# A transformer kernel: shift and scale of the second norm multiplied out on GpSimd in place of TensorE and VectorE

## The chip, the core and the metric

The kernel runs on one core of a Trainium2 chip. Its engines work side by side, each through its own queue in a fixed order, and wait for one another by semaphores: TensorE (PE, with its weight loads shown apart as PEld), VectorE (DVE), ScalarE (ACT), GpSimd (POOL) and SyncE (SP), whose queue issues the weight transfers. The metric is the device time of one launch in microseconds (us), as the median of repeated runs.

## What is computed

Two transformer blocks over 256 tokens of width 1024, all in 32-bit floats. The part that matters here is the modulation of the first block: a vector `c` gives six rows of 1024 numbers, and the fourth and fifth (index 3 and 4) are shift and scale of the second norm, which stands ahead of the mixture of experts.

```
mod = silu(c) @ w_ada + b_ada
shift1, scale1, gate1, shift2, scale2, gate2 = split(mod, 6)
h  = rms_norm(x, norm1_g) * (1 + scale1) + shift1
q, k, v, ..., g_sb, g_mb = split(h @ w_in)
x  = x + gate1 * ((sigmoid(g_sb) * (o_sb @ w_branch_sb) + sigmoid(g_mb) * (o_mb @ w_branch_mb)) @ w_out)
h2 = rms_norm(x, norm2_g) * (1 + scale2) + shift2
x  = x + gate2 * moe_ffn(h2)          # router, 64 experts, a shared expert
```

After it come a norm and the second block (two feed-forward parts around a mixing part), which the change doesn't touch.

## The kernel before

The first block's dense part is `phase_a`. Its matrix products are split into a high and a low part on both sides: for each 128-row chunk of a weight matrix, ACT rounds it (wH, L125), DVE subtracts (wL, L126), and PE multiplies three times (L116 to L118). The results of the projections are the tiles `pslt` (transposed) and `pslin`.

One part of the modulation is a product of a 1024-vector with a 1024 x 1024 matrix. `ada_half(q, j, E)` (L367) makes half of it, 512 columns: it loads the 512 columns of `w_ada` as two tiles `wada` of four chunks each, and then takes one of two ways. For every q but 4, PE multiplies (L383): 8 products of a chunk with a stationary tile `cpad` that holds silu(c) in one of 32 columns, into `psada`, and ACT copies the result to `adaE` (L385). For q = 4 DVE does it alone: one multiplication (L376) and seven multiply-adds (L378) of a 128 x 512 chunk by a number for each partition, accumulated in `adaE`. Either way the 128 partitions of `adaE` still have to be summed: `ada_column` (L387) does that for q = 3 and q = 4 by eight products with a column of ones (`psac`, L397), and DVE adds the bias (L399) to give `sh2` (shift, q = 3) or `sc2` (scale, q = 4). There is one buffer `adaE`; `ada_rows(2)`, which makes gate1, uses it just before `ada_column(3)`.

Weights go through a ring of 7 slots of 8 KB for each partition. SP issues the loads in the order of the program, and each waits until the slot's last contents have been read. The loads around the change are, in this order: four `wada` tiles for gate1, four for shift (q = 3), eight `win` tiles for the four gate projections, four `wada` tiles for scale (q = 4), four `wbr` tiles (branch products) and four `wout` tiles. With seven slots, the fourth to seventh `win` tiles go where the four `wada` tiles of q = 3 lay.

`weave` mixes streams of work. One woven group holds the projections of q, k, v of the second attention, `ada_rows(2)` and `ada_column(3)`, beside the first attention. The next holds the four gate projections (192 `pslin` products in all) and `ada_column(4)`, beside the second attention in four pairs of heads: scores (`psms`, L868 and L869), maximum (mbm), exponential, division, transposes (`psmp`, L891) and values (`psmo`, L853 and L855). A scheduler then sets the order of each engine's instructions but SP's, when the program is built. At run time each engine follows that order.

DVE uses `sh2` from L636 on and `sc2` in L485 and L639, for the router's weights. Then come the branch products, the output projection, the router, gate2 (`ada_rows(5)`) and the experts.

Of the kernel before, what the change touches and what calls it, by code (L numbers as in the profile page):

```python
# [11 lines left out]
F32 = mybir.dt.float32  # L12
# [3 lines left out]
ALU = mybir.AluOpType  # L16
# [4 lines left out]
P = 128  # L21
# [83 lines left out]
class Net:  # L105
# [261 lines left out]
    def ada_half(self, q, j, E):  # L367

        nc = self.nc
        w = self.w_chunk(self.a["w_ada"], q * D + j * 512, 512, "wada")  # L370
        if q == 4:
            E = E[:, j * 512:(j + 1) * 512]
            for k in range(8):
                c, wk = self.csilu[:, k:k + 1], w(k, 1)[:, 0]
                if k == 0:
                    nc.vector.tensor_scalar(E, wk, c, None, op0=ALU.mult)  # L376
                else:
                    nc.vector.scalar_tensor_tensor(E, wk, c, E, op0=ALU.mult, op1=ALU.add)  # L378
            return
        ps = self.ps.tile([P, 512], F32, tag="wk", name="psada")  # L380
        for kk in range(2):
            for g in range(4):
                nc.tensor.matmul(ps[32 * g:32 * g + 32], self.cpad[:, 4 * kk + g, :], w(4 * kk + g, 1)[:, 0],  # L383
                                 start=kk == 0, stop=kk == 1)
        nc.scalar.copy(E[:, j * 512:(j + 1) * 512], ps)  # L385
# [1680 lines left out]
```

## Time and profile before

| what | us |
|---|---|
| median of 3 runs | 1320.99 (1320.15 to 1322.29) |
| the profiled execution | 1318.1 |
| its span, first to last instruction | 1316.3 |
| PE busy | 1231.2 |
| DVE busy | 700.9 |
| ACT busy | 550.9 |
| GpSimd busy | 36.8 |

The times of single instructions below are those of the profiled execution, counted from the start of its span. A group's mean is over all its instructions; the idle time beside it is of its engine, and the name behind an arrow is what ended that.

### The profile page before, as it was taken

To read this page: it belongs to the slowest core of one execution; us is meant where nothing else is said; L and a number is where in the kernel's file an instruction comes from. 1 tells how busy PE (TensorE), PEld (TensorE's weight loads), DVE (VectorE), ACT (ScalarE), POOL (GpSimd) and SP (SyncE) were. 2 spreads that over 40 slices of the span, in tenths; PEclk is the share of its full clock that TensorE was granted. 3 is DMA by queue.
4 is the path that set the end of the run, shared out by engine and by line. 5 is a ranking of instruction groups with operands and counts; after the bars stand their busy time and mean duration, and the time that the engine had idled before them with its cause. 6 is when DMAs were issued, how large, how long until landed. Compare 5 with 4: busy or idle time off the path is not lost. (4 is left out here: it accounts for less than half of the span.)

```text
span 1316.3 us, 19900 instructions
## 1 busy us (share of the span) xinstructions
PE 1231.2 (94%) x7245; PEld 835.5 (63%) x7245; DVE 700.9 (53%) x1562; ACT 550.9 (42%) x1056; POOL 36.8 (3%) x43
## 2 busy tenths in 40 slices
PE   5999999987899989989989999999999998999997
PEld 4886788765444434434424437888877965788885
DVE  3565697863244333323322329666769766756664
ACT  2465565632222111112111117556745664555662
POOL 0000000000000000000000000000012021000000
PEclk9999899988899999989989999999999999999999
DMA  9875757688899999999999994955385145095610
GB/s 334 268 257 194 270 177 277 199 311 316 325 402 409 408 408 408 408 410 408 409 407 409 374 386 139 339 186 206 132 216 170 33 31 186 18 367 186 212 64 33
DMA packets 155140, 351.85 MB, mean 267 GB/s; under 512 B 14688, under 2 KB 69920, under 8 KB 155040
## 3 DMA queue, kind: packets, MB, share of 16 engines
q1 hardware_dynamic: 152816, 347.25, 71.7%
q0 software_dynamic: 1328, 3.16, 2.3%
q8 instruction: 58, 0.95, 0.3%
q14 instruction: 42, 0.34, 0.1%
q10 hardware_dynamic: 896, 0.15, 0.1%
HBM read 349.46 MB, written 1.06 MB: 266 GB/s over the span
## 5 line engine op out<-in xcount | busy, mean ns | idle before, releaser
L1331 PE MATMUL psgu<-wgu,xg 128*32 128x512 f32 x1600 | 221.1, 627 | 34.9 <-DMA wgu<-in_w_up_e_dram 33.0
L1331 PEld LDWEIGHTS psgu<-wgu,xg 128*32 128x32 f32 x1600 | 64.9, 114 | 182.8 <-issue 156.2
L1552 DVE SCALAR_TENSOR_TENSOR wL<-wgu,ffn_pre_g,wH 128x512 fp32r<-128x512 f32 x160 | 119.0, 750 | 74.8 <-ACT wH L1551 73.2
L1551 ACT ACTIVATE wH<-wgu,ffn_pre_g 128x512 fp32r<-128x512 f32 x160 | 114.4, 724 | 80.7 <-PE psgu L117 72.9
L116 PE MATMUL psgu<-wH,Hc 128*128 128x512 f32 x320 | 126.2, 394 | 0.0
L118 PE MATMUL psgu<-wL,Hc 128*128 128x512 f32 x320 | 124.8, 390 | 0.0
L117 PE MATMUL psgu<-wH,Lc 128*128 128x512 f32 x320 | 124.7, 390 | 0.0
L1338 DVE SCALAR_TENSOR_TENSOR act<-act,ws,psgu 128x256 f32<-128x256 f32 x25 | 12.0, 481 | 199.9 <-ACT act L1337 199.9
L1337 ACT ACTIVATE act<-psgu 128x256 f32<-128x256 f32 x25 | 9.6, 385 | 213.0 <-PE psgu L1331 213.0
L1355 PE MATMUL psdn<-wdn,aT 128*32 128x512 f32 x800 | 94.6, 595 | 2.3 <-DMA wdn<-in_w_down_e_dram 2.1
L125 ACT CAST wH<-gt 128x512 fp32r<-128x512 f32 x61 | 37.6, 618 | 107.1 <-DVE gt L1191 103.4
L118 PEld LDWEIGHTS psgu<-wL,Hc 128*128 128x128 f32 x320 | 60.0, 188 | 12.7
L126 DVE TENSOR_TENSOR wL<-win,wH 128x512 fp32r<-128x512 f32 x80 | 53.4, 687 | 27.5 <-ACT wH L125 24.6
L117 PEld LDWEIGHTS psgu<-wH,Lc 128*128 128x128 f32 x320 | 60.1, 188 | 12.1
L116 PEld LDWEIGHTS psgu<-wH,Hc 128*128 128x128 f32 x320 | 60.1, 188 | 12.0
L125 ACT CAST wH<-win 128x512 fp32r<-128x512 f32 x80 | 47.8, 617 | 35.3 <-PE pslt L118 20.0
L126 DVE TENSOR_TENSOR wL<-gt,wH 128x512 fp32r<-128x512 f32 x61 | 42.1, 691 | 35.6 <-ACT wH L125 35.3
L1355 PEld LDWEIGHTS psdn<-wdn,aT 128*32 128x32 f32 x800 | 24.5, 109 | 54.2 <-issue 43.7
L1305 ACT ACTIVATE xg<-psga,sh,gs 128x256 f32<-128x256 f32 (+1 forms) x52 | 28.9, 557 | 70.8 <-PE psga L1304 70.7
L1303 PE MATMUL psga<-Pt,xH 128*128 128x256 f32 (+1 forms) x208 | 54.1, 298 | 4.2 <-DVE Pt L1281 4.2
L126 DVE TENSOR_TENSOR wL<-wdn,wH 128x512 fp32r<-128x512 f32 x64 | 44.0, 692 | 21.4 <-ACT wH L125 9.8
L1304 PE MATMUL psga<-Pt,xL 128*128 128x256 f32 (+1 forms) x208 | 52.0, 289 | 0.0
(555 smaller groups left out, 2562.7 us busy)
## 6 DMA issues: line engine op xcount, KB each, us to landing
wgu<-in_w_gate_e_dram SPq DMA_DIRECT2D x128, 512.0 KB, 12.0
wgu<-in_w_up_e_dram SPq DMA_DIRECT2D x128, 512.0 KB, 11.2
wdn<-in_w_down_e_dram SPq DMA_DIRECT2D x62, 1024.0 KB, 12.1
wgu<-in_ffn_w_gu_dram SPq DMA_DIRECT2D x88, 512.0 KB, 7.1
win<-in_w_in_dram SPq DMA_DIRECT2D x26, 1024.0 KB, 9.6
wada<-in_w_ada_dram SPq DMA_DIRECT2D x24, 1024.0 KB, 6.1
wdn<-in_ffn_w_down_dram SPq DMA_DIRECT2D x22, 1024.0 KB, 10.4
wout<-in_w_out_dram SPq DMA_DIRECT2D x8, 1024.0 KB, 13.1
```

The source lines that it names most:

```text
L116: mm(ps, lH, rH, start=start, stop=False, skip_group_check=True)
L117: mm(ps, lL, rH, start=False, stop=False, skip_group_check=True)
L118: mm(ps, lH, rL, start=False, stop=stop, skip_group_check=True)
L125: self.nc.scalar.copy(H, raw)
L126: self.nc.vector.tensor_sub(L, raw, H.bitcast(F32))
L1303: mm(o, xH[:, tt, k + kk], pt, start=kk == 0 and tt == 0, stop=False, skip_group_check=True)
L1304: mm(o, xL[:, tt, k + kk], pt, start=False, stop=kk == 1 and tt == 1, skip_group_check=True)
L1305: nc.scalar.activation(B.xg[:, k, :w], ps[:, 0, :w], AF.Identity, scale=self.gs2[:, k:k + 1], bias=self.sh2[:, k:k + 1])
L1331: mm(ps[q:q + 32], xg[:, k, i * P + q:i * P + q + 32], W[e][:, :, k % 4, :], start=k == 0, stop=k == 7)
L1355: mm(ps[q:q + 32], aT[:, f, q:q + 32], wd[e][:, f, sl], start=f == 0, stop=f == 1)
L1551: self.nc.scalar.activation(H, raw, AF.Copy, scale=g)
L1552: self.nc.vector.scalar_tensor_tensor(L, raw, g, H.bitcast(F32), op0=ALU.mult, op1=ALU.subtract)
```

## The change

For q = 3 and q = 4, GpSimd now multiplies the chunks and accumulates them. What DVE did in one multiply-add is two instructions on GpSimd, a multiplication into a new tile `adaT` (one buffer) and an addition to `adaE`. For q = 3 the products on PE and the copies on ACT are gone, for q = 4 the instructions on DVE. The sum over partitions (L397 of before) stays on PE.

```
-        if q == 4:
+        if q in (3, 4):
             E = E[:, j * 512:(j + 1) * 512]
             for k in range(8):
                 c, wk = self.csilu[:, k:k + 1], w(k, 1)[:, 0]
                 if k == 0:
-                    nc.vector.tensor_scalar(E, wk, c, None, op0=ALU.mult)
+                    nc.gpsimd.tensor_scalar(E, wk, c, None, op0=ALU.mult)
                 else:
-                    nc.vector.scalar_tensor_tensor(E, wk, c, E, op0=ALU.mult, op1=ALU.add)
+                    t = self.pa.tile([P, 512], F32, tag="adaT", name="adaT")
+                    nc.gpsimd.tensor_scalar(t, wk, c, None, op0=ALU.mult)
+                    nc.gpsimd.tensor_tensor(E, E, t, op=ALU.add)
             return
```

Lines behind L379 of before have numbers higher by 2 in the changed kernel. The scheduler also sets other orders on the engines. On PE, around the sum over partitions of q = 3 (`psac`), this stood before (the two `psada` rows are the second half of q = 3, the `psms` rows scores of the first two pairs of heads, `pslin` the first gate projection):

```order
L383 MATMUL psada_1263<-wada_1259,cpad_137 32x512 x4
L383 MATMUL psada_1263<-wada_1261,cpad_137 32x512 x4
L868 MATMUL psms_1290<-km_96,qm_95 128x128
L869 MATMUL psms_1290<-km_96,qm_95 128x256
L868 MATMUL psms_1297<-km_96,qm_95 128x128
L397 MATMUL psac_1273<-ones_70,adaE_1230 128x1 x8
L869 MATMUL psms_1297<-km_96,qm_95 128x256
L868 MATMUL psms_1307<-km_96,qm_95 128x128
L869 MATMUL psms_1307<-km_96,qm_95 128x256
L868 MATMUL psms_1314<-km_96,qm_95 128x128
L869 MATMUL psms_1314<-km_96,qm_95 128x256
L116 MATMUL pslin_1325<-wH_1327,hH_91 128x512
```

and this stands in the changed kernel, behind the 8 `psms` products, 12 `psmp` transposes and 8 `psmo` products of the first two pairs of heads (the rows start in the scores of the last two pairs):

```order
L870 MATMUL psms_1534<-km_96,qm_95 128x128
L871 MATMUL psms_1534<-km_96,qm_95 128x256
L870 MATMUL psms_1541<-km_96,qm_95 128x128
L871 MATMUL psms_1541<-km_96,qm_95 128x256
L870 MATMUL psms_1551<-km_96,qm_95 128x128
L871 MATMUL psms_1551<-km_96,qm_95 128x256
L870 MATMUL psms_1558<-km_96,qm_95 128x128
L871 MATMUL psms_1558<-km_96,qm_95 128x256
L399 MATMUL psac_1297<-ones_70,adaE_1230 128x1 x8
L116 MATMUL pslin_1349<-wH_1351,hH_91 128x512
L117 MATMUL pslin_1349<-wH_1351,hL_92 128x512
L118 MATMUL pslin_1349<-wL_1352,hH_91 128x512
```

The sum for q = 3 has moved behind the first two pairs' whole attention and the last two pairs' scores, and all 192 products of the gate projections stand behind it. Before, those pieces of the attention were spread between the gate projections. The sum for q = 4 stands behind the last gate projection and ahead of the branch products in both kernels.

On GpSimd's queue this stood from the first bias transfer of the second attention (`t5bias`) on, before:

```order
L792 DMA t5scr_724<-t5row_721 8x384
L797 DMA t5bias_1287<-t5scr_724 128x2x256
L797 DMA t5bias_1304<-t5scr_724 128x2x256
L797 DMA t5bias_1507<-t5scr_724 128x2x256
L797 DMA t5bias_1524<-t5scr_724 128x2x256
L934 DMA xh_67<-in_final_g_dram 128x1024
```

and this now, where `wada_1231` and `wada_1233` are the tiles of the first half of q = 3 and `wada_1271` the first of the second half:

```order
L799 DMA t5bias_1328<-t5scr_724 128x2x256
L379 TENSOR_SCALAR adaT_1236<-wada_1231,cpad_137 128x512
L376 TENSOR_SCALAR adaE_1230<-wada_1231,cpad_137 128x512
L376 TENSOR_SCALAR adaE_1230<-wada_1271,cpad_137 128x512
L380 TENSOR_TENSOR adaE_1230<-adaE_1230,adaT_1236 128x512
L379 TENSOR_SCALAR adaT_1239<-wada_1231,cpad_137 128x512
L380 TENSOR_TENSOR adaE_1230<-adaE_1230,adaT_1239 128x512
L379 TENSOR_SCALAR adaT_1242<-wada_1231,cpad_137 128x512
L380 TENSOR_TENSOR adaE_1230<-adaE_1230,adaT_1242 128x512
L799 DMA t5bias_1531<-t5scr_724 128x2x256
L379 TENSOR_SCALAR adaT_1245<-wada_1233,cpad_137 128x512
L380 TENSOR_TENSOR adaE_1230<-adaE_1230,adaT_1245 128x512
```

The 30 instructions for q = 3 stand around the last two `t5bias` transfers, and the 30 for q = 4 behind those. Each addition waits for the multiplication ahead of it, and each multiplication into `adaT` for the addition that read that buffer last.

On SP's queue the loads stand in the same order. What the third to eighth `win` tile of the gate projections wait for, before (besides the DMA semaphore, the engine that read the slot last):

```order
L197 DMA win_1447<-in_w_in_dram 128x4x512 [waits DMAHW6_49,PE_49]
L197 DMA win_1449<-in_w_in_dram 128x4x512 [waits DMAHW7_49,PE_49]
L197 DMA win_1601<-in_w_in_dram 128x4x512 [waits DMAHW0_49,PE_49]
L197 DMA win_1603<-in_w_in_dram 128x4x512 [waits DMAHW1_49,PE_49]
L197 DMA win_1723<-in_w_in_dram 128x4x512 [waits DMAHW2_49,PE_49]
L197 DMA win_1725<-in_w_in_dram 128x4x512 [waits DMAHW3_49,DVE_49]
```

and now:

```order
L197 DMA win_1471<-in_w_in_dram 128x4x512 [waits DMAHW6_49,PE_49]
L197 DMA win_1473<-in_w_in_dram 128x4x512 [waits DMAHW7_49,Pool_49]
L197 DMA win_1625<-in_w_in_dram 128x4x512 [waits DMAHW0_49,Pool_49]
L197 DMA win_1627<-in_w_in_dram 128x4x512 [waits DMAHW1_49,Pool_49]
L197 DMA win_1747<-in_w_in_dram 128x4x512 [waits DMAHW2_49,Pool_49]
L197 DMA win_1749<-in_w_in_dram 128x4x512 [waits DMAHW3_49,DVE_49,Activation_49]
```

Four of the eight tiles now wait for GpSimd.

## Rows read from the trace of the kernel before

**Rows 1.** The page, parts 1 and 2: busy times; PE's busy tenths.
```profile
PE 1231.2 (94%) x7245; PEld 835.5 (63%) x7245; DVE 700.9 (53%) x1562; ACT 550.9 (42%) x1056; POOL 36.8 (3%) x43
...
PE   5999999987899989989989999999999998999997
```
**Rows 2.** Timeline of PE: start us, us, instruction; merged where the count exceeds 1.
```profile
129.53 1.92 PE L383 MATMUL psada<-wada,cpad 128*32 128x512 f32 x14
...
132.18 1.92 PE L383 MATMUL psada<-wada,cpad 128*32 128x512 f32 x16
...
134.88 3.96 PE L397 MATMUL psac<-ones,adaE 128*128 128x1 f32 x16
...
141.21 0.79 PE L116 MATMUL pslin<-wH,hH 128*128 128x512 f32 x1
...
151.31 1.47 PE L891 MATMUL psmp<-ident,mbat 128*128 128x128 f32 x12
...
159.33 0.44 PE L855 MATMUL psmo<-mbat,vm 128*64 128x128 f32 x4
...
163.67 0.70 PE L869 MATMUL psms<-km,qm 64*128 64x256 f32 x4
...
195.48 3.74 PE L397 MATMUL psac<-ones,adaE 128*128 128x1 f32 x16
```
**Rows 3.** Stretch of the gate projections, instructions of the tile pslin alone.
```profile
141.20:195.50 54.30, 47.05 (x192) 36.91 (x192) 2.05 (x3) 2.28 (x4) 0.96 0.56 188
```
**Rows 4.** SP's waits from 200 to 300: waiter, waited for, us, times, longest.
```profile
SPq L209 <- PE psada L383: 16.7, 2, 12.5
```
**Rows 5.** Groups of DVE from 141.2 to 195.5: busy us, mean ns.
```profile
L126 DVE TENSOR_TENSOR wL<-win,wH 128x512 fp32r<-128x512 f32 x28 | 18.6, 685 | 6.5 <-ACT wH L125 5.4 <-PE pslin L117 1.0
L378 DVE SCALAR_TENSOR_TENSOR adaE<-wada,cpad,adaE 128x512 f32<-128x512 f32 x14 | 10.3, 740 | 0.0
...
L376 DVE TENSOR_SCALAR adaE<-wada,cpad 128x512 f32<-128x512 f32 x2 | 1.0, 478 | 0.0
```
**Rows 6.** Groups of GpSimd over the span: busy us, mean ns.
```profile
L1850 POOL TENSOR_TENSOR G<-G,win 128x768 f32<-128x768 f32 x4 | 7.9, 1972 | 40.8 <-DMA win<-in_window_dram 23.2 <-DMA G<-in_na_rpb_dram 17.6
L1558 POOL TENSOR_SCALAR row<-row 128x1024 f32<-128x1024 f32 x2 | 5.5, 2774 | 650.2 <-DMA row<-in_ffn_post_g_dram 650.2
L2015 POOL TENSOR_TENSOR sq<-sq,sqt 128x256 f32<-128x256 f32 x6 | 5.0, 834 | 55.1 <-ACT sqt L2013 55.1
L797 POOL DMA_DIRECT2D t5bias<-t5scr x4 | 3.0, 739 | 67.1 <-DVE mbm L874 61.2 <-issue 5.9
```
**Rows 7.** Timeline of GpSimd: single instructions beside work of DVE.
```profile
999.08 2.40 POOL L1850 TENSOR_TENSOR G<-G,win 128x768 f32<-128x768 f32 x1 [7.30 <-DMA G<-in_na_rpb_dram]
...
1101.41 1.34 POOL L2015 TENSOR_TENSOR sq<-sq,sqt 128x256 f32<-128x256 f32 x1 [10.24 <-ACT sqt L2013]
...
1185.08 2.77 POOL L1558 TENSOR_SCALAR row<-row 128x1024 f32<-128x1024 f32 x1 [79.40 <-DMA row<-in_ffn_post_g_dram]
```
**Rows 8.** Timeline of DVE at three of these places.
```profile
999.04 0.74 DVE L1552 SCALAR_TENSOR_TENSOR wL<-win,mix_pre_g,wH 128x512 fp32r<-128x512 f32 x1
...
1000.15 1.89 DVE L1552 SCALAR_TENSOR_TENSOR wL<-win,mix_pre_g,wH 128x512 fp32r<-128x512 f32 x1
...
1186.45 0.75 DVE L1552 SCALAR_TENSOR_TENSOR wL<-wgu,ffn_pre_g,wH 128x512 fp32r<-128x512 f32 x1 [0.57 <-ACT wH L1551]
```
**Rows 9.** Timeline of DVE: the last reader of gate1's adaE.
```profile
127.58 0.69 DVE L413 TENSOR_TENSOR adaL<-adaE,adaH 128x512 fp32r<-128x512 f32 x1 [2.67 <-ACT adaH L412]
```
**Rows 10.** Timeline of SP's queue: the last shift tile's load, first and last scale tile's.
```profile
119.38 0.37 SPq L197 DMA_DIRECT2D wada<-in_w_ada_dram  x1
...
149.99 0.37 SPq L197 DMA_DIRECT2D wada<-in_w_ada_dram  x1
...
174.42 0.37 SPq L197 DMA_DIRECT2D wada<-in_w_ada_dram  x1
```
**Rows 11.** The tile wada: time from a load's issue to its landing.
```profile
DMA to landing us min/median/max: 5.0/6.1/15.8
```

## The prediction

> **What bounds the kernel now.** I read the page's busy times first: PE works 94% of the span and GpSimd 3% [rows 1]. The work moved goes from the fullest engine to the emptiest, so the share alone would promise a gain. But a share is a mean over stages, and PE follows a fixed order. So the second view is PE's timeline around the change [rows 2]. It shows two fences: the sum over partitions (psac) of q = 3 starts at 134.9, right behind its products, and the first gate projection (pslin) at 141.2. The sum of q = 4 starts at 195.5, right behind the last gate projection. Between them PE has no gap: the gate projections' 192 products hold 47.1 of 54.3 us [rows 3], and most of the rest is the attention's small products. In this stage PE is the bound, and DVE's multiply-adds for q = 4 are off its path. Third, what comes after hangs on this stage: SP's queue waits 16.7 us for the product of gate2's ada, which PE reaches later in the same fixed order, before it issues expert loads [rows 4]. A delay of PE here therefore shifts the rest.
>
> **What is removed.** For q = 3: 32 PE passes in two groups of 1.92 us, 3.8 us together [rows 2]. They are on PE's path. For q = 4: on DVE 10.3 + 1.0 us [rows 5], beside PE's work, so worth nothing by itself. Two copies on ACT go too; they only feed the psac that now waits for something else.
>
> **What is added: the price of one instruction.** No row shows a 128 x 512 multiplication or addition on GpSimd. Multiplication: 1024 elements took 2774 ns [rows 6], half of that is 1.39 us, which I take, as the same operation on the same engine. Addition: with the disturbed ones of rows 7 taken out, 256 elements take (6 x 834 - 1340) / 5 = 0.73 us and 768 take (4 x 1972 - 2400) / 3 = 1.83 us [rows 6, 7]; 512 lies midway, 1.28 us. A pair is then 2.67 us, where DVE took 0.74 us [rows 5].
>
> To this comes what GpSimd waits for. The two disturbed additions were longer by 0.57 and 0.61 us, and DVE was in an instruction with two SBUF inputs each time. Such a DVE instruction is held as well: L1552 at 1000.15 took 1.89 us instead of 0.74, beside the addition from 999.08 [rows 7, 8]. A GpSimd multiplication did not hold it: at 1186.45 it took 0.75 us inside the 2.77 us of L1558 [rows 7, 8]. So only additions collide. Two of ten were hit, by about 0.6 us; DVE's splits alone fill 18.6 of 54.3 us here [rows 5]. I add 0.25 us a pair for q = 3, where DVE has less to do, and 0.35 for q = 4. Lower bound: nothing. Upper bound: every addition waits for a whole split (0.69 us) and 0.2 us more for handing over between dependent instructions, 0.9 together.
>
> **Shift (q = 3).** GpSimd waits for the one adaE buffer, which DVE reads last for gate1 at 127.6 + 0.7 = 128.3 [rows 9]. The loads are no limit: the last is issued at 119.4 and lands 6.1 us later [rows 10, 11]. One multiplication runs before that into adaT. Behind it stand 15 multiplications (20.8 us), 14 additions (17.9), two t5bias issues of 0.74 us (1.5) [rows 6] and 14 x 0.25 = 3.5 us of collisions: 43.7 us, done at 172.0 (168.5 to 181.1). PE, having done the attention pieces that stand ahead in the new order, waits. Before, those took from 134.1, where psada ends, to 164.4 with gate projections among them [rows 2], so PE is at psac by about 160 at the latest and stands idle for 12 us there, besides gaps before. Then psac itself, 4.0 us as before [rows 2]: gate projections start at 176.0 instead of 141.2, 34.8 us late (31.3 to 43.9). Queued behind this wait are all 192 products on PE, and on DVE (behind the bias addition that reads psac) the second attention's divisions and further weight splits. On SP four gate loads wait for GpSimd, the last until about 172; PE needs that tile only after three projections, some 35 us after it starts, so I cost this at nothing.
>
> **The stretch between.** The attention pieces that moved ahead no longer lie in it: 1.5 us of transposes, 1.6 of value products and 1.7 of scores (start and duration of the last merged rows [rows 2]), 4.7 together. So it takes 49.6 us, and PE reaches the psac of q = 4 at 225.6.
>
> **Scale (q = 4).** The first scale tile can be loaded when the first gate projection's second tile is used up: 149.99 against 141.2 before, 8.8 us after the start [rows 2, 10], and it lands 6.1 us later: 190.9. The last was issued 33.2 us after the start, so lands at 215.3, and isn't needed before 225. GpSimd then needs 16 x 1.39 + 14 x 1.28 + 14 x 0.35 = 45.1 us: 236.0. PE waits 10.4 us more. The psac of q = 4 starts at 236.0 instead of 195.5: **40.5 us late**. With the low bounds of both columns it is 187.4 + 40.2 = 227.6, 32 us late; with the high ones 200.0 + 52.8 = 252.8, 57 us late. The orders behind that are the same in both kernels, and PE has no slack there to give back. The 3.8 us removed are already inside, since the start of the gate projections is computed anew.
>
> **Two rules weighed.** Apart from the sum: the Trainium skill, "GPSIMD Engine Reference", section 4.1 "Engine selection", advises VectorE for elementwise work and calls one-input operations on GpSimd about line-rate, and its section 3.1 gives 769 ns for a 512-element loop at best. The row on L1558 (2.71 ns an element) disagrees. By that figure, called an estimate, a multiplication would be 0.77 us and the whole 18 us late instead of 40; this is the first rival's direction. The Trainium skill, "SBUF — State Buffer", section "Who interferes with whom", says that a DVE instruction with two SBUF inputs contends with any GpSimd instruction that reads SBUF. The trace agrees for additions and not for the multiplication; by the rule as it stands the multiplications collide too, which is the second rival.
>
> **The rivals.** First, *short multiplications*: 0.48 us, as DVE's own L376 [rows 5], and no collisions. Then shift is ready 15 x 0.48 + 17.9 + 1.5 = 26.6 us after 128.3, at 154.9, the projections start at 158.9, scale is ready at 158.9 + 14.9 + 25.6 = 199.4, before PE gets there at 208.5: 13 us late, 1334. Against it stands the one multiplication row. Second, *every GpSimd instruction collides*: in the scale column 30 x 0.69 = 20.7 us, in the shift column half as much. Shift 178.9, projections 182.9, scale 182.9 + 14.9 + 40.2 + 20.7 = 258.7: 63 us late, 1384. Against it: L1552 inside L1558. Third, on the other side, *the delay is given back*: if the expert stream, and not PE's order, set when the experts begin, phase A could be late behind it, and only PE's 3.8 us would be left as a gain: 1317, at most no change. It decides if the first expert load does not depend on work behind the second psac. Rows 4 speak against it, since that load waits for PE's gate2 product. That the change doesn't do what it says is out: the 60 instructions stand on GpSimd's queue.
>
> **How the numbers follow.** The profiled execution took 1318.1 us, 1.8 more than its span and 2.9 less than the median of 1321.0. The shift is added to either: 1318.1 + 40.5 = 1358.6 for an execution like it, 1321.0 + 40.5 = 1361.5 for the median, which I give, as 1362. Chances: forecast 0.75 (its own range 1353 to 1378), short multiplications 0.10, collisions everywhere 0.11, given back 0.04. For 8 in 10 I reach from 1340 (between forecast and first rival) to 1384 (the second rival). A measurement can tell about 0.2%, 2.6 us, from no change. The forecast and the first two rivals are slower, 0.96; the third splits into 0.02 faster and 0.02 same.
>
> **What would show it.** In the changed profile: GpSimd nearly without a gap from 128 to about 172 and from about 191 to 236, with multiplications near 1.4 us and additions near 1.3; two waits of PE on psac, released by GpSimd's last addition, the first over 10 us; gate projections starting near 176; the second psac near 236; the same distance from there to the end as before. The forecast is wrong if a pair takes well under 2.4 us or over 3.6, if PE does not wait at the second psac, or if the experts start less late than the second psac.

## The result and the profile after

The changed kernel takes **1370.14 us** (median of four, 1368.26 to 1372.55) against 1320.68 for the kernel before: a ratio of 1.037 with a 95% interval from 1.035 to 1.039, 49.5 us slower. Slower was forecast, by 40.5 us; the time lies in the forecast's own range. The profiled span grew by 50.2 us, from 1316.3 to 1366.5.

The page of the changed kernel, parts 1 and 2 (engine, busy us, share, instructions; then tenths in 40 slices), answers to [rows 1]:
```profile
PE 1228.6 (90%) x7213; PEld 836.1 (61%) x7213; DVE 703.0 (51%) x1546; ACT 548.4 (40%) x1052; POOL 129.9 (10%) x103
...
PE   5998286898789998989997998999999999999997
...
POOL 0003949100000000000000000000011012000000
```
PE does 2.6 us less work and stands idle 52.8 us longer. The holes in its row are in the fifth and the seventh slice (34.2 us each), where GpSimd's row is nearly full: the work went to an empty engine, and the full one waits for it.

Where it waits is on its timeline (start us, us, instruction, and in brackets the idle time ahead and what ended it), the answer to [rows 2]:
```profile
146.68 0.59 PE L871 MATMUL psms<-km,qm 64*128 64x256 f32 x2
174.25 3.96 PE L399 MATMUL psac<-ones,adaE 128*128 128x1 f32 x16 [26.98 <-POOL adaE L380]
178.08 0.78 PE L116 MATMUL pslin<-wH,hH 128*128 128x512 f32 x1
...
226.72 0.39 PE L118 MATMUL pslin<-wL,hH 128*128 128x512 f32 x1
244.04 3.96 PE L399 MATMUL psac<-ones,adaE 128*128 128x1 f32 x16 [16.93 <-POOL adaE L380]
```
The first fence stands at 174.25 instead of 134.88, the second at 244.04 instead of 195.48: 48.6 us late. The list of waits between 100 and 260 us (waiter, waited for, us, times, longest) puts 43.9 us on these two places:
```profile
PE psac L399 <- POOL adaE L380: 43.9, 2, 27.0
DVE sh L401 <- PE psac L399: 28.6, 1, 28.6
```
DVE stands 28.6 us behind the first, with the attention's divisions and the weight splits queued after it.

GpSimd's own timeline shows both columns:
```profile
128.22 3.11 POOL L376 TENSOR_SCALAR adaE<-wada,cpad 128x512 f32<-128x512 f32 x2 [22.93 <-DVE adaL L415]
...
171.29 1.56 POOL L379 TENSOR_SCALAR adaT<-wada,cpad 128x512 f32<-128x512 f32 x1
172.94 1.26 POOL L380 TENSOR_TENSOR adaE<-adaE,adaT 128x512 f32<-128x512 f32 x1
192.45 1.66 POOL L376 TENSOR_SCALAR adaE<-wada,cpad 128x512 f32<-128x512 f32 x1 [18.25 <-DMA wada<-in_w_ada_dram]
...
205.31 2.40 POOL L379 TENSOR_SCALAR adaT<-wada,cpad 128x512 f32<-128x512 f32 x1
...
242.72 1.26 POOL L380 TENSOR_TENSOR adaE<-adaE,adaT 128x512 f32<-128x512 f32 x1
```
The shift column lasts from 128.22 to 174.2, the scale column from 192.45 to 243.98, both almost without a gap. PE's two waits end with them.

### The profile page after: what moved, and what is told of

The parts are those of the page before. It is cut to its first block, busy times and chain, and to the rows that moved or that the text cites. A ratio compares the mean times of both kernels' runs of the same rounds, so it can differ in the third digit from the quotient of the medians.

```text
span 1366.5 us, 19890 instructions
## 1 busy us (share of the span) xinstructions
PE 1228.6 (90%) x7213; PEld 836.1 (61%) x7213; DVE 703.0 (51%) x1546; ACT 548.4 (40%) x1052; POOL 129.9 (10%) x103
## 5 line engine op out<-in xcount | busy, mean ns | idle before, releaser
L126 DVE TENSOR_TENSOR wL<-win,wH 128x512 fp32r<-128x512 f32 x80 | 61.1, 782 | 33.8 <-ACT wH L125 31.1
L1560 POOL TENSOR_SCALAR row<-row 128x1024 f32<-128x1024 f32 x2 | 5.6, 2808 | 651.1 <-DMA row<-in_ffn_post_g_dram 651.1
```

The source lines that it names most:

```text
L126: self.nc.vector.tensor_sub(L, raw, H.bitcast(F32))
```

## The experiments

Theory W, which the prediction gave: the price is the length of the two columns on GpSimd, paid where PE's fixed order meets them. The rival C: GpSimd's work disturbs DVE, whose splits feed PE, and that is where the time goes. A second question was whether the work costs anything on GpSimd when nobody waits for it.

**One column alone.** The scale column on GpSimd, the shift as before; then the reverse.
```
-        if q in (3, 4):        # the changed kernel
+        if q == 4:             # scale only
```


> Only scale (q = 4) on GpSimd; shift (q = 3) on TensorE as before, and PE's order is that of before. Theory of the waits (the time goes where PE stands at the sum over partitions, psac, until GpSimd's last addition): the first scale tile lands near 156, GpSimd needs about 51 us as in the changed kernel, so the second psac starts near 207 instead of 195.5: 10 to 14 us slower than before, 1331 to 1335. Theory of contention (GpSimd's instructions and the ring slots they hold slow DVE's splits and the loads, the waits only show it): the gate projections themselves get longer by a fifth or more, and the loss is half of the change's 49 us, about 25, 1345.

> Only shift (q = 3) on GpSimd; scale (q = 4) on VectorE as before; PE's order is that of the changed kernel. Theory of the waits: gate projections start near 178 as in the changed kernel, then PE runs through to the second psac near 228, which finds its input ready: 32 to 34 us slower than before, 1353 to 1355. Theory of contention: GpSimd is idle beside the gate projections, so only what happens before 174 is left, and half of the loss, about 25 us, 1346.

Measured: scale only 1333.78 us, ratio 1.010 [1.008, 1.013]; shift only 1353.25 us, ratio 1.024 [1.020, 1.029]. That is 13 to 14 us and about 33 us, together 47 of the 49.5 us. PE's sums in the first kernel:
```profile
206.91 3.96 PE L399 MATMUL psac<-ones,adaE 128*128 128x1 f32 x16 [9.21 <-POOL adaE L380]
```
and in the second:
```profile
175.14 3.96 PE L408 MATMUL psac<-ones,adaE 128*128 128x1 f32 x16 [26.75 <-POOL adaE L389]
178.97 0.78 PE L116 MATMUL pslin<-wH,hH 128*128 128x512 f32 x1
...
228.10 3.74 PE L408 MATMUL psac<-ones,adaE 128*128 128x1 f32 x16
```
With scale alone the second sum is 11.4 us late against [rows 2]; with shift alone it is 32.6 us late and waits for nothing. Each column is paid at its own fence, and the time follows the second fence.

**Half the length.** Both columns on GpSimd, with four of the eight chunks of each half; the other four are left out, so the sums are incomplete.
```
-            for k in range(8):
+            for k in range(4):
```


> The changed kernel with four of the eight chunks of each half left out, so GpSimd does half the work and the sums are incomplete. Theory of the waits: GpSimd ends shift near 151, gate projections start near 155 (13 us late), scale is done near 197, before PE arrives near 209, so only the first wait is left: 12 to 15 us slower than before, 1333 to 1336. A loss in proportion to GpSimd's work would be 25 us, 1345.

Measured: 1332.27 us, ratio 1.011 [1.007, 1.014], about 13 us over before and not half of 49.5. PE's sums:
```profile
149.34 3.96 PE L399 MATMUL psac<-ones,adaE 128*128 128x1 f32 x16 [18.62 <-POOL adaE L380]
...
208.25 3.74 PE L399 MATMUL psac<-ones,adaE 128*128 128x1 f32 x16
```
The first is 14.5 us late, the second waits for nothing. Half the work costs a quarter, because the price is what sticks out beyond PE's other work, and the first part of a column is covered. A charge per instruction would have given about 25 us.

**The sums moved back.** All of GpSimd's work stays, the shift has its own tile, and both sums over partitions are written behind the gate projections, so that the first fence is gone.
```
-        E = self.pa.tile([P, D], F32, tag="adaE", name="adaE", bufs=1)
+        E = self.gate2 if q == 3 else self.pa.tile([P, D], F32, tag="adaE", name="adaE", bufs=1)
...
+        self.sums.append((out, q, E))
...
+            for u in self.sums:
+                self.ada_sum(*u)
```


> All of GpSimd's work as in the change, but shift accumulates in the still unused gate2 tile, so that it need not wait for adaE, and both sums over partitions stand behind the gate projections. Theory of the waits: gate projections start near 132, PE reaches the sums near 183 and waits only for scale, done near 203; 8 to 14 us slower than before, 1329 to 1335. Theory of contention: the same GpSimd work lies beside the same stage, so the loss stays above 30 us, over 1350.

Measured: 1344.39 us, ratio 1.018 [1.013, 1.022], some 25 us over before: half of the price is gone, but twice what I expected is left. SP's queue and GpSimd show what I left out: first SP's waits from 120 to 157 us and the loads, then the first scale multiplication, then PE's second sum:
```profile
SPq L197 <- POOL adaT L379: 23.1, 2, 13.8
```
```profile
155.51 20.90 SPq L197 DMA_DIRECT2D wada<-in_w_ada_dram  x4
```
```profile
167.42 1.56 POOL L376 TENSOR_SCALAR adaE<-wada,cpad 128x512 f32<-128x512 f32 x1 [10.12 <-DMA wada<-in_w_ada_dram]
```
```profile
217.87 3.96 PE L405 MATMUL psac<-ones,adaE 128*128 128x1 f32 x16 [15.87 <-POOL adaE L380]
```
The scale's tiles stand behind the gate projections' weights in SP's queue, and four of those weights' tiles take the slots that the shift's multiplications free one after another. For the last of these SP waits 13.8 us. So the scale's first load is issued at 155.51, when the shift column is nearly through (it ends at 155.8), whatever PE does. The second fence then has to wait for two columns in a row.

**GpSimd's work where nobody waits.** The kernel before, with 32 added instructions whose results nobody reads on GpSimd beside the gate projections: once all multiplications, once two multiplications and 30 additions.
```
+            u = self.pa.tile([P, 512], F32, tag="idle", name="idle")
+            nc.gpsimd.tensor_scalar(u, w(0, 1)[:, 0], self.csilu[:, 0:1], None, op0=ALU.mult)
+            for i in range(15):
+                nc.gpsimd.tensor_scalar(u, u, self.csilu[:, 0:1], None, op0=ALU.mult)   # or tensor_tensor(u, u, u, op=ALU.add)
```


> The kernel before, with 32 added multiplications of 128 x 512 on GpSimd (16 behind each half of the scale's loads, from about 156 to 208) whose results nothing uses; PE's order is that of before. Theory of the waits: no engine waits for them, so the time stays within 3 us of before, 1316 to 1323. Theory of contention: the same stage gets slower by 6 us or more. On the port: if multiplications do not collide with DVE (the prediction's reading), they take 1.56 us each throughout and DVE's splits (L126 of win) stay at 685 ns; if they do, their mean is over 1.8 us and the splits are longer.

> As e5, with 30 additions of 128 x 512 in place of 30 of the 32 multiplications, from about 156 to 200. Theory of the waits: within 3 us of before. Theory of contention: 6 us or more slower. On the port: additions are held by DVE's splits and hold them, so their mean is over 1.45 us instead of 1.26, and the splits beside them (L126 of win) take 0.75 us or more in the mean.

Measured: multiplications 1322.41 us, ratio 1.002 [1.000, 1.003]; additions 1337.09 us, ratio 1.013 [1.011, 1.015]. W held for the first and fell for the second, where C was right: 16 us for results that nobody reads. GpSimd's groups (busy us, mean ns) of the two kernels:
```profile
L375 POOL TENSOR_SCALAR idle<-idle,cpad 128x512 f32<-128x512 f32 x30 | 52.2, 1739 | 2.8
```
```profile
L375 POOL TENSOR_TENSOR idle<-idle 128x512 f32<-128x512 f32 x30 | 38.3, 1278 | 2.4
```
The same five weight splits on DVE, first beside the multiplications, then beside the additions:
```profile
172.56 3.50 DVE L126 TENSOR_TENSOR wL<-win,wH 128x512 fp32r<-128x512 f32 x5
```
```profile
178.26 6.46 DVE L126 TENSOR_TENSOR wL<-win,wH 128x512 fp32r<-128x512 f32 x5
```
In the kernel before they take 3.08 us:
```profile
171.91 3.08 DVE L126 TENSOR_TENSOR wL<-win,wH 128x512 fp32r<-128x512 f32 x5
```
DVE's groups from 157 to 200 us, beside the multiplications and beside the additions, show the rest (the kernel before: multiply-adds 740 ns, multiplication 478 [rows 5]):
```profile
L382 DVE SCALAR_TENSOR_TENSOR adaE<-wada,cpad,adaE 128x512 f32<-128x512 f32 x14 | 14.0, 1003 | 0.0
L380 DVE TENSOR_SCALAR adaE<-wada,cpad 128x512 f32<-128x512 f32 x2 | 1.6, 804 | 0.0
```
```profile
L382 DVE SCALAR_TENSOR_TENSOR adaE<-wada,cpad,adaE 128x512 f32<-128x512 f32 x7 | 9.7, 1395 | 0.0
L380 DVE TENSOR_SCALAR adaE<-wada,cpad 128x512 f32<-128x512 f32 x2 | 2.5, 1258 | 0.0
```
Additions without a gap double DVE's two-input instructions and keep their own 1.28 us. Multiplications lengthen DVE's less, these five splits by a seventh and the multiply-adds by a third, and are lengthened themselves, from 1.56 to 1.74 us. DVE's one-input multiplication of a weight chunk is held too, by either. In the kernel with the additions, DVE has no free time left from 160 to 200, and PE waits for a split:
```profile
191.74 0.79 PE L118 MATMUL pslin<-wL,hH 128*128 128x512 f32 x1 [3.86 <-DVE wL L126]
```
So C is real, but on PE it isn't what cost the 49.5 us. In the changed kernel additions alternate with multiplications, DVE no longer has its own multiply-adds there, and the gate projections take 49.0 us (178.08 to 227.1), no longer than forecast. With shift only, where GpSimd stands idle beside them, they take 49.1 us (178.97 to 228.1). With scale only, in the order of before, PE does wait for a split once:
```profile
173.38 0.73 PE L118 MATMUL pslin<-wL,hH 128*128 128x512 f32 x2 [3.04 <-DVE wL L126]
```
But it then stands 9.2 us at the fence all the same, so that wait isn't paid. What GpSimd and DVE cost each other in the changed kernel is in the length of the columns, 6.7 us in the scale's (below).

**The work off the path.** The shift on GpSimd in its own tile, the scale on DVE as before, both sums late; then the same with the shift on DVE too.
```
+        if q == 3:             # first kernel: GpSimd; q == 4 is VectorE's again
...
+        self.sums.append((out, q, E))
```
```
-        if q == 4:             # the kernel before
+        if q in (3, 4):        # second kernel: both on VectorE
...
+        self.sums.append((out, q, E))
```


> Shift on GpSimd, accumulated in the unused gate2 tile from 103 on, scale on VectorE as before, both sums over partitions behind the gate projections. Theory of the waits: GpSimd is done near 155, long before PE gets to the sums, so nothing waits; PE starts the gate projections near 134 instead of 141 and is spared 3.8 us: 0 to 5 us faster than before, 1315 to 1321. Theory of contention, with the slots that GpSimd holds until 155: loads of the scale tiles start near 155, DVE ends them late and the splits suffer: 5 to 15 us slower, 1325 to 1335.

> As e7, with shift on VectorE too (one multiplication and seven multiply-adds of 0.74 us a half, 11.4 us in all), so GpSimd has none of it. Theory of the waits: DVE has the room, and PE is spared 3.8 us and the early sum: 2 to 7 us faster than before, 1313 to 1318. If e7 loses and this does not, it is GpSimd's slowness (slots, port) and not the order that costs in e7. If DVE has no room around 105 to 145, its splits come late and this is no faster than before.

Measured: 1325.65 us, ratio 1.003 [1.002, 1.005], and 1325.05 us, ratio 1.004 [1.003, 1.005]. I expected both to be faster, by PE's 3.8 us of removed products; both are 4 to 5 us slower. The first keeps half of the changed kernel's work on GpSimd and takes 28 us less than shift only did with its sum in the old place. Two things differ between these two: the tile of its own, whose worth in the changed kernel comes next, and the place of the sum; what they take away is the wait. Since the second kernel, without GpSimd, loses as much, the loss isn't GpSimd's. PE's timeline shows where it is. PE starts the gate projections 6 to 7 us earlier, runs ahead of the splits and waits for them, 6.3 us in four places in the first kernel (1.2 of them for ACT's rounding ahead of a split) and 4.9 us in one in the second; the kernel before has no such wait there. Here are the longest wait and the two sums of the first kernel, then of the second:
```profile
138.71 0.74 PE L118 MATMUL pslin<-wL,hH 128*128 128x512 f32 x2 [2.96 <-DVE wL L126]
...
195.39 3.74 PE L414 MATMUL psac<-ones,gate 128*128 128x1 f32 x16
198.99 3.94 PE L414 MATMUL psac<-ones,adaE 128*128 128x1 f32 x16
202.79 0.78 PE L116 MATMUL pslin<-wH,h2a 128*128 128x512 f32 x1
```
```profile
141.65 1.22 PE L118 MATMUL pslin<-wL,hH 128*128 128x512 f32 x2 [4.93 <-DVE wL L126]
...
194.81 3.74 PE L403 MATMUL psac<-ones,gate 128*128 128x1 f32 x16
198.41 3.94 PE L403 MATMUL psac<-ones,adaE 128*128 128x1 f32 x16
202.21 0.77 PE L116 MATMUL pslin<-wH,h2a 128*128 128x512 f32 x1
```
In the kernel before, the next product behind its one sum:
```profile
199.08 0.41 PE L641 MATMUL psre<-wre,ones 128*128 128x64 f32 x2
```
So PE reaches the sums no more than 0.7 us ahead of before (195.48) and has two of them to do, 32 one-column products in a row, where the kernel before has one left: it is through 3.7 and 3.1 us later. The 5 us right behind the sums, of the kernel before, of the one with the shift on GpSimd and of the one with both on DVE, add a little (busy us and instructions of each engine, granted clock as a share of full speed, DMA share, GB/s):
```profile
199.20:204.20 5.00, 5.00 (x18) 3.97 (x18) 2.23 (x5) 2.30 (x4) 0.00 (x0) 0.66 1.05 386
```
```profile
203.00:208.00 5.00, 5.00 (x12) 3.90 (x13) 2.63 (x9) 0.75 (x2) 0.00 (x0) 0.50 1.05 386
```
```profile
202.40:207.40 5.00, 5.00 (x14) 3.91 (x15) 2.65 (x9) 0.98 (x2) 0.00 (x0) 0.58 1.05 387
```
Against full clock before loses 0.34 x 5 = 1.7 us here, the other two 2.5 and 2.1. That makes 4.5 and 3.5 us of the 4 to 5. So PE's lead, and with it the 3.8 us of removed products, went into waits for the splits; why these come no earlier no run here tests.

**The wait for a tile.** The changed kernel with one edit: the shift gathers in the second gate's tile, which is free then, so GpSimd need not wait 22.93 us for DVE's last use of adaE.
```
-        E = self.pa.tile([P, D], F32, tag="adaE", name="adaE", bufs=1)
+        E = self.gate2 if q == 3 else self.pa.tile([P, D], F32, tag="adaE", name="adaE", bufs=1)
```


> The changed kernel with one edit: the shift's sum is gathered in the tile of the second gate, which is free at that time, and no longer in adaE. In the changed kernel's trace GpSimd's second instruction on the shift starts at 128.22, after 22.93 us in which it waited for VectorE's last use of adaE. Theory W (the price is the length of the two columns from where each starts): the shift starts at 104, and with the collisions of that stretch is done at 156 to 160 (the kernel with the late shift did the same column in 52.4 us), its products with ones follow at 158 and not at 174.25, the scale's first tile lands about 16 us earlier than 192.45, and the scale is done near 227 to 230 and not at 243.98: 14 to 18 us faster than the changed kernel, 1352 to 1356. Rival (the scale's tiles come through SyncE's queue behind the gate projections' weights, and these hang on VectorE's splits, so the end of the scale stays where it is): 1366 to 1370.

Measured: 1352.23 us, ratio 1.023 [1.019, 1.026]: 18 us of the changed kernel's time, as W expected. PE's sums:
```profile
153.23 3.96 PE L399 MATMUL psac<-ones,gate 128*128 128x1 f32 x16 [19.96 <-POOL gate L380]
...
226.55 3.96 PE L399 MATMUL psac<-ones,adaE 128*128 128x1 f32 x16 [6.47 <-POOL adaE L380]
```
The column started at 102.94 and was done at 153.2, earlier than I had said; the second fence came at 226.55 instead of 244.04, 17.5 us earlier. A third of the price was a buffer.

**The additions on DVE.** The changed kernel with the 28 additions on VectorE.
```
-                    nc.gpsimd.tensor_tensor(E, E, t, op=ALU.add)
+                    nc.vector.tensor_tensor(E, E, t, op=ALU.add)
```


> The changed kernel with one edit: the 28 additions are VectorE's, the 32 multiplications stay on GpSimd. Theory W (GpSimd's length sets the time): a column is 16 multiplications of 1.56 to 2.41 us, 26 to 38 us and not the 45.9 (from 128.22) and 51.5 of the changed kernel; the shift is done at 156 to 160, the scale's first tile lands some 15 us earlier, and the scale is done at 206 to 213, about when TensorE gets to it: 30 to 38 us faster than the changed kernel, 1332 to 1340. Rival (the two engines hold each other up, and the price goes where the additions go: VectorE's 28 additions of 0.66 to 1.1 us put its splits late, and TensorE waits for these in place of the sums): less than half of that gain, 1353 or more.

Measured: 1356.74 us, ratio 1.027 [1.024, 1.031]. The gain of 13 us is what the rival allowed, but not by its mechanism: VectorE's additions took 0.69 us, undisturbed. GpSimd's timeline and then PE's show two other waits:
```profile
134.81 1.56 POOL L379 TENSOR_SCALAR adaT<-wada,cpad 128x512 f32<-128x512 f32 x1 [0.82 <-DVE adaE L380]
```
```profile
153.07 1.29 PE L893 MATMUL psmp<-ident,mbat 128*128 128x128 f32 x4 [20.74 <-DVE mbat L886]
```
There is one adaT buffer, so each multiplication waits 0.82 us for VectorE's addition, and a pair still takes 2.4 us instead of 3.0. And VectorE, whose queue is in order, stands behind each product of GpSimd, with the attention's divisions (mbat) queued after it, for which PE then waits 20.7 us. Neither theory had that.

No version here beats the kernel before.

## Why the prediction was right, and by how much it missed

**What bounds the kernel.** Right. Two waits of PE, each ended by GpSimd's last addition, hold 43.9 us, the first over 10 us as said. It was 27.0 us and not 12, since PE was through with the attention's pieces at 147.3 and not at about 160; the sum doesn't use that, because the wait ends with GpSimd either way. From the second fence to the end it was 1120.8 us before and is 1122.5 now. So the delay is neither given back nor multiplied. The 1.7 us more fit PE's clock: after a wait of 16.9 us and 16 one-column products the granted clock was at its lower level (0.50 of full speed, 1.2 of 2.4 GHz) for longer than before (0.66 in the row above), in these stretches of the changed kernel:
```profile
248.00:252.00 4.00, 4.00 (x12) 3.23 (x12) 1.89 (x5) 1.79 (x3) 0.00 (x0) 0.50 0.49 138
252.00:256.00 4.00, 4.00 (x15) 3.17 (x14) 1.13 (x3) 1.24 (x2) 0.00 (x0) 0.72 0.64 257
```
That is 0.50 x 4 + 0.28 x 4 = 3.1 us lost against 1.7 us.

**The price of an instruction: the term that was mis-sized.** The addition was right: 1.26 us undisturbed, forecast 1.28. The multiplication takes 1.56 us and not the 1.39 I had from halving L1558's 1024 elements [rows 6]; halving leaves out a fixed part, by an estimate from these two rows some 0.35 us. GpSimd's groups of the changed kernel from 190 to 246 us, the scale column (busy us, mean ns of one, idle time ahead):
```profile
L379 POOL TENSOR_SCALAR adaT<-wada,cpad 128x512 f32<-128x512 f32 x14 | 26.2, 1872 | 1.2
L380 POOL TENSOR_TENSOR adaE<-adaE,adaT 128x512 f32<-128x512 f32 x14 | 18.9, 1347 | 1.2
L376 POOL TENSOR_SCALAR adaE<-wada,cpad 128x512 f32<-128x512 f32 x2 | 4.2, 2094 | 18.3 <-DMA wada<-in_w_ada_dram 18.3
```
The 16 multiplications took 30.4 us against 22.2 forecast (2.7 of the 8.2 from the base, the rest from being held), the additions 18.9 against 17.9 + 4.9 of collisions, and the gaps between dependent instructions, 0.08 us each, come to 2.2 us that I costed at nothing. Together 51.5 against 45.1. That the sum missed by no more is partly luck: of the 4.9 us charged to the additions 1.0 was used, and the other 3.9 stood in for half of what the multiplications took beyond their forecast.

**"So only additions collide": this step was wrong.** It rested on a single multiplication, inside which DVE's instruction was not held [rows 7, 8]; it did not ask whether the multiplication itself was. The kernel before had a second one (852.83 to 855.61), and inside that one of two splits did take longer, 0.86 us where the other took 0.69:
```profile
853.55 0.86 DVE L126 TENSOR_TENSOR wL<-wdn,wH 128x512 fp32r<-128x512 f32 x1 [0.67 <-ACT wH L125]
```
In the changed kernel it is above all the multiplications that are longer, many of them 1.88 or 2.40 us, while the additions hold DVE and mostly keep their length (12 of the scale's 14 took 1.26 to 1.31 us, two 1.75 and 1.77). Two splits from 134.56, the first of them beside the addition from 134.30, take 2.15 us instead of 1.29:
```profile
134.56 2.15 DVE L126 TENSOR_TENSOR wL<-win,wH 128x512 fp32r<-128x512 f32 x2
```
The Trainium skill, "SBUF — State Buffer", section "Who interferes with whom", says that a DVE instruction with two SBUF inputs contends with any GpSimd instruction that reads SBUF; the multiplications agree with it now as well, though they are longer by only 0.13 us (shift) and 0.31 us (scale) on average.

**The rest of the sum.** The shift was done at 174.2 instead of 172.0 for the same reasons (46.0 us against 43.7). The stretch between took 49.0 us (forecast 49.6), and the first scale tile came 14.4 us after the projections' start (14.9). So at the second fence: 2.1 late from the shift (the projections started at 178.1 instead of 176.0), 0.5 early from the tile, 6.4 late from the scale column, 8.0 in all (244.04 against 236.0); with the 1.7 us of clock that makes the 9.7 us between 40.5 and the 50.2 by which the span grew.

**The rivals.** *Short multiplications* fell: 1.56 us, not 0.48. *The delay is given back* fell with the two distances above. *Every GpSimd instruction collides* was half right: multiplications are held too, but being held added 5.4 us to the scale's multiplications and 1.3 to its additions where the rival had 20.7, and a pair stayed at 3.2 us, under the 3.6 that I had named as the limit. The handing over, which the sum left at nothing, measured 0.16 us a pair, inside its bound of 0.2.

## What to carry to other kernels

Before work goes to an idle engine, find the instruction that consumes its last result on the engine that sets the time, and compare the length of the whole chain with what stands in order ahead of that instruction: only what sticks out is paid, and it is paid in full. The shift on GpSimd cost 33 us in front of a fence. With a tile of its own and its sum behind the projections it cost no more than the same order with the shift on DVE (1325.65 and 1325.05 us). Look also for the buffer that the chain must wait for before it can start; here it was worth 18 us.

## What the runs showed of the hardware that I had not expected

- GpSimd and DVE hold each other up unequally. Beside 30 additions in a row DVE's two-input splits took 1.29 us each instead of 0.62 (6.46 and 3.08 us for five) and the additions kept 1.28 us; beside 30 multiplications the splits took 0.70 us, DVE's multiply-adds 1.00 instead of 0.74, and the multiplications 1.74 instead of 1.56 us. DVE's one-input multiplication of 128 x 512 was held as well, 1.26 us beside additions and 0.80 beside multiplications instead of 0.48.
- Useless work on an idle engine cost 16 us of 1320 when it was additions and about 2 us when it was multiplications, though these were busy longer (52.2 against 38.3 us).
- Behind 32 one-column products in a row, through which PE was busy all the while, the granted clock was 0.50 and 0.58 of full speed over 5 us; behind the 16 of the kernel before it was 0.66.
